# RWKV chain that keeps only the state's products: products with V and of the outputs moved into batches outside the chain

## The chip, the cores and the metric

One core of one Trainium2 chip runs the whole program, two chained transformer blocks. The metric is the time of one execution in microseconds (us) on the device; the median of several runs is taken. A core has a matrix engine (PE, TensorE), a vector engine (DVE), a scalar engine (ACT), a general engine (POOL) and a sequencer that starts most of the transfers (SP). Each runs its own list of instructions in order, and waits on semaphores where it needs another's result. A matmul writes into PSUM (8 banks of 128 partitions x 2 KB), from where DVE or ACT copy the result to SBUF.

## The reference, cut to what matters

Block 1 and the rest of block 2 are the same before and after. What the change touches is the RWKV-7 time mix of block 2: 8 heads of 64, two directions d, 512 tokens. Per head and direction a 64x64 state is carried over the tokens:

```
def step(state, inp):
    r_t, w_t, k_t, v_t, a_t, b_t = inp
    sa = jnp.einsum('dbhij,dbhj->dbhi', state, a_t)
    state = (state * w_t[..., None, :] + sa[..., :, None] * b_t[..., None, :]
             + v_t[..., :, None] * k_t[..., None, :])
    y = jnp.einsum('dbhij,dbhj->dbhi', state, r_t)
    return state, y
...
_, ys = lax.scan(step, s0, xs)
...
y = ys[0] + jnp.flip(ys[1], axis=1)
mu = jnp.mean(y, axis=-1, keepdims=True)
var = jnp.mean(jnp.square(y - mu), axis=-1, keepdims=True)
y = ((y - mu) * lax.rsqrt(var + GN_EPS)).reshape(bsz, t, c) * lnx_w + lnx_b
...
out = (y + bonus.reshape(bsz, t, c)) * g
```

## The kernel before, in words

`block2` does the scan in chunks of 64 tokens: 8 chunks, and 4 pairs of heads p = 0 to 3. The two heads of a pair, e = 0 and 1, lie on partitions 0 to 63 and 64 to 127. For each pair the program is written in four parts.

- `prep(p)` (from L1046) makes, from the projected r, k, v and gates, the chunk matrices: Z (128 columns a chunk: those of a and of r), BK (b and k), its transpose BKT, and the products pP = BK x Z (L1128, one matmul of 64 rows x 128 columns a chunk, head and direction), which DVE masks into M (L1130). So M holds what tokens of a chunk do to later ones of the same chunk. The strictly triangular blocks of M go out to memory (scL, L1135) and come back in another layout, as LF (L1150) and XH (L1152). There DVE inverts them: 30 rows, two instructions each (L1158 the products sx, L1160 their sum into XH). This is called the recursion below.
- fill: GEMM groups of later use (the gates of block 2, the next pair's projections, and for p = 3 the qkv projection, L1315), issued with low priority.
- `finish(p)` (from L1163) sends the inverses out (scX, L1169) and back into M (L1174), transposes (pax, L1182) and multiplies them together (pt1 L1189, pg2 L1194). LF's buffer holds its operand, so the LF of the next pair is loaded only when `finish(p)` is through.
- `chain(p)`: V is transposed (pvs, L1204) into VU, M x V of every chunk is made at once (pv, L1215), and 8 steps follow, one chunk a direction. A step is: pw = Z x state (L1229); DVE adds M x V (L1231, w); pu = M x w (L1234); ACT and DVE copy a head each into VU (L1000); then in px the old state times the identity (L1241) plus BKT x [V, U] (L1243); ACT scales one direction into the new state S (L1264), DVE the other (L1265). Each step also makes its output py from S and VU (L1250, L1252), copied by ACT (L1256) or added by DVE (L1258). Group norm, the gate and the store follow (to L1299).

A matmul of this f32 kind is one instruction in the program and two in the profile. The fills' and qkv's operands are float32r and are one in both.

What sets the order of the work: a list scheduler places all instructions of these parts, each engine's list apart, before the program runs, by priority, readiness by its own costs and free buffers. Fill has the lowest priority and goes where a chain's matmul is not ready. The order is fixed when the program is built. PSUM: pool `pg` (tag g, 2 banks) and `pa_` (tag a, 2), `ps_` (s, 2), `pc_` (y and c, one each). A qkv group needs both banks of g and both of a; `finish(p)` uses the banks of a (for p = 3 those of s).

Times below call f0, f1, f2, f3 the ends of the last pg2 matmul of each `finish` and "attention" the start of block 2's attention (paS, L1388).

Of the kernel before, what the change touches and what calls it, by code (L numbers as in the profile page):

```python
# [17 lines left out]
S = 512  # L18
# [138 lines left out]
class Ker:  # L157
# [806 lines left out]
    def block2(self, out):  # L964
# [79 lines left out]
        def prep(p):  # L1044
# [36 lines left out]
            for d in range(2):  # L1081
# [37 lines left out]
                for hf in ((0, 1), (1, 0))[d]:  # L1119
                    cs = slice(4 * hf, 4 * hf + 4)  # L1120
                    Z[hf] = rk.tile([128, 4, 128], F32, tag=f"Z{d}", name=f"Z{p}{d}{hf}", bufs=4)
                    nc.vector.tensor_tensor(Z[hf][:, :, 0:64], perm(kn, 64)[:, cs], perm(prv, 66)[:, cs], ALU.mult)
                    ve.tensor_tensor(Z[hf][:, :, 64:128], c8(r_)[:, cs], inc[:, cs], ALU.mult)  # L1123
                    for e in range(2):
                        rr = slice(64 * e, 64 * e + 64)
                        pp = ps_.tile([128, 4, 128], F32, tag="s", name=f"pP{p}{d}{hf}{e}")
                        for i in range(4):
                            nc.tensor.matmul(pp[:, i, :], BK[rr, 4 * hf + i, :], Z[hf][rr, i, :], start=True, stop=True)  # L1128
                        mk = rmask[d].rearrange("p (o t) -> p o t", o=2)[:, e:e + 1]
                        nc.vector.tensor_tensor(M[e][:, d, cs], pp, mk.to_broadcast([128, 4, 128]), ALU.mult)  # L1130
# [66 lines left out]
        def chain(p, st, u, PCs, XH, LF, M):  # L1197
            Y = rl.tile([128, 8, 64], F32, tag="Y", name=f"Y{p}")
            vt = V[p]
            VU = rl.tile([128, 8, 128], F32, tag="VU", name=f"VU{p}")  # L1200
            for h in range(2):
# [15 lines left out]
            Sn = None
            for s in range(8):
                cd = (s, 7 - s)
                zs = [st[d][0][cd[d] // 4][:, cd[d] % 4, :] for d in range(2)]  # L1220
                So = Sn
                pcb = pc_.tile([128, 512], F32, tag="c", name=f"pcb{p}{s}")
                pw, pu, px = [pcb[:, 128 * i:128 * i + 128].rearrange("p (d v) -> p d v", d=2) for i in range(3)]
                w = W0[:, 0, s, :]
                w = bass.AP(w.tensor, w.offset, [list(w.ap[0]), [512 + (7 - 2 * s) * 64, 2], [1, 64]])
                if s > 0:
                    for d in range(2):
                        for e in range(2):
                            nc.tensor.matmul(pw[O[e], d, :], zs[d][H[e], 0:64], So[H[e], d, :], start=True, stop=True)  # L1229
# [15 lines left out]
                def ymm():  # L1245
                    py = pc_.tile([128, 2, 64], F32, tag="y", name=f"py{p}{s}")
                    for d in range(2):
                        for e in range(2):
                            if s > 0:
                                nc.tensor.matmul(py[H[e], d, :], zs[d][H[e], 64:128], So[H[e], d, :], start=True, stop=False)  # L1250
                        for e in range(2):
                            nc.tensor.matmul(py[H[e], d, :], M[e][:, d, cd[d], 64:128], VU[:, cd[d], H[e]], start=s == 0, stop=True)  # L1252
                    b = Y[:, s, :]
                    yv = bass.AP(b.tensor, b.offset, [list(b.ap[0]), [(7 - 2 * s) * 64, 2], [1, 64]])
                    if s < 4:
                        nc.scalar.activation(yv, py, AF.Copy)  # L1256
                    else:
                        nc.vector.tensor_tensor(yv, py, yv, ALU.add)  # L1258
# [16 lines left out]
            yt = W0[:, 0].rearrange("p c v -> p (c v)")  # L1275
# [164 lines left out]
        st = prep(0)  # L1440
        fill(W[0], 5)
        finish(0, *st)
        chain(0, *st)
        st = prep(1)
        fill(W[1], 8)
        finish(1, *st)
# [185 lines left out]
```

## Time and profile before

| what | value |
|---|---|
| runs, median | 1834.92, 1851.11, 1856.5 us; 1851.11 us |
| profiled execution: time, span | 1853.1 us, 1851.3 us |
| PE busy, mean granted clock | 1763.1 us (95% of the span), 0.957 |
| DVE, ACT, POOL busy | 1108.2, 780.1, 207.6 us |
| f0, f1, f2, f3, attention | 945.2, 1016.8, 1122.7, 1210.7, 1276 us from the span's start |

In the rows, "busy" of an engine is the time that its instructions took, and x the number of instructions. PE overlaps its matmuls, so that a row's duration is longer than the distance to the next row's start: paces are read from start to start. PEclk is the granted clock as a share of 2.4 GHz: 1.00 is 2.4 GHz, 0.50 is 1.2 GHz, and values between are stretches with some of both. PEld are the weight loads beside the matmuls.

### The profile page before, as it was taken

Reading aid. Unit: us, or ns where it says so; the run is one execution under the profiler, and the core shown is the slowest. Engines: PE = TensorE matmul, PEld = TensorE weight load, DVE = VectorE, ACT = ScalarE, POOL = GpSimd, SP = SyncE. Lnnn points to the kernel's source line nnn. Section 1 sums busy time; section 2 is a strip of 40 time slices with the busy share of each in tenths; the row PEclk is TensorE's granted clock in tenths of the full one; section 3 lists DMA queues with packets and bytes.
Section 4 is the critical chain, followed back from the end, with each engine's and each line's share of the span. In section 5 each row is a group of like instructions: output and inputs, shape, how many; then the busy total and the mean of one; then the engine's idle time right before and its main releaser. Section 6 shows DMA issues by size and latency. Waiting matters only on the chain.

```text
span 1851.3 us, 30948 instructions
## 1 busy us (share of the span) xinstructions
PE 1763.1 (95%) x11888; PEld 1481.1 (80%) x11888; DVE 1108.2 (60%) x2311; ACT 780.1 (42%) x1559; POOL 207.6 (11%) x238
## 2 busy tenths in 40 slices
PE   8999989999999999897789998999999999999998
PEld 7787877889989999776667767876678888888887
DVE  5765786787734777855746682436556553355445
ACT  6552547654433446543233331235434442234333
POOL 1100130200000003442212121112000000000000
PEclk9999999999999999988689997689999999999999
DMA  5221324543333325622122122112055333333333
GB/s 170 59 52 47 83 54 154 160 126 92 92 97 92 92 86 164 179 68 58 46 66 58 44 63 71 39 33 92 18 185 157 103 93 96 97 91 97 96 92 131
DMA packets 130676, 170.83 MB, mean 92 GB/s; under 512 B 44456, under 2 KB 59056, under 8 KB 130529
## 3 DMA queue, kind: packets, MB, share of 16 engines
q1 hardware_dynamic: 130528, 168.87, 31.9%
q8 instruction: 93, 1.52, 0.3%
q14 instruction: 55, 0.44, 0.1%
HBM read 155.19 MB, written 13.63 MB: 91 GB/s over the span
## 4 chain that ended last, share of the span: by engine, by line
PE 83%; DVE 7%; DMA 4%; issue 3%; ACT 2%; POOL 1%; SPq 0%; DVEq 0%; POOLq 0%; ACTq 0%
PE ps_w_ff L251 19%; PE ps_w_ffn_in L251 13%; PE ps_w_in L284 6%; PE ps_w_in L251 6%; PE ps_w_ffn_out L251 6%; PE ps_qkv L1315 3%; PE ps_w_out L251 2%; PE pP L1128 2%; PE ps_w_ple_gate L251 2%; DMA XH<-scL 1%; PE ps_w_up_attn L251 1%; PE py L1252 1%; PE paS L1388 1%; PE ps_first L364 1%; PE ps_w_o L266 1%
## 5 line engine op out<-in xcount | busy, mean ns | idle before, releaser
L203 DVE TENSOR_TENSOR wl_w_ff<-raw_w_ff,wh_w_ff 128x512 fp32r<-128x512 f32 x128 | 88.2, 689 | 131.7 <-ACT wh_w_ff L202 131.6
L202 ACT ACTIVATE wh_w_ff<-raw_w_ff 128x512 fp32r<-128x512 f32 x128 | 80.9, 632 | 194.8 <-PE ps_w_ff L251 186.1
L203 POOL TENSOR_TENSOR wl_w_in<-raw_w_in,wh_w_in 128x512 fp32r<-128x512 f32 x60 | 81.9, 1370 | 260.0 <-ACT wh_w_in L202 191.8
L202 ACT ACTIVATE wh_w_in<-raw_w_in 128x512 fp32r<-128x512 f32 (+1 forms) x118 | 72.9, 622 | 89.9 <-PE ps_w_in L284 38.2
L202 ACT ACTIVATE wh_w_ffn_in<-raw_w_ffn_in 128x512 fp32r<-128x512 f32 x96 | 59.9, 630 | 101.5 <-PE ps_w_ffn_in L251 88.0
L251 PE MATMUL ps_w_ff<-Yl,wh_w_ff 128*128 128x512 f32 x256 | 101.0, 395 | 0.0
L251 PE MATMUL ps_w_ff<-Yh,wh_w_ff 128*128 128x512 f32 x256 | 101.0, 395 | 0.0
L251 PE MATMUL ps_w_ff<-Yh,wl_w_ff 128*128 128x512 f32 x256 | 101.0, 395 | 0.0
L251 PE MATMUL ps_w_ffn_out<-Y_hi,wl_w_ffn_out 128*128 128x256 f32 (+1 forms) x256 | 83.5, 326 | 2.2 <-DVE wl_w_ffn_out L203 2.1
L251 PE MATMUL ps_w_ffn_out<-Y_hi,wh_w_ffn_out 128*128 128x256 f32 (+1 forms) x256 | 83.7, 327 | 0.0
L251 PE MATMUL ps_w_ffn_out<-Y_lo,wh_w_ffn_out 128*128 128x256 f32 (+1 forms) x256 | 83.4, 326 | 0.0
L203 DVE TENSOR_TENSOR wl_w_ffn_in<-raw_w_ffn_in,wh_w_ffn_in 128x512 fp32r<-128x512 f32 x96 | 65.7, 689 | 20.4 <-ACT wh_w_ffn_in L202 19.4
L251 PE MATMUL ps_w_ffn_in<-fa_hi,wl_w_ffn_in 128*128 128x258 f32 x352 | 74.3, 285 | 2.0 <-DVE wl_w_ffn_in L203 2.0
L251 PE MATMUL ps_w_ffn_in<-fa_hi,wh_w_ffn_in 128*128 128x258 f32 x352 | 74.1, 285 | 1.9 <-ACT wh_w_ffn_in L202 1.9
L203 DVE TENSOR_TENSOR wl_w_ffn_out<-raw_w_ffn_out,wh_w_ffn_out 128x512 fp32r<-128x512 f32 (+1 forms) x72 | 47.4, 662 | 47.2 <-ACT wh_w_ffn_out L202 46.4
L251 PE MATMUL ps_w_ffn_in<-fb_hi,wl_w_ffn_in 128*128 128x258 f32 x352 | 74.3, 285 | 0.2 <-DVE wl_w_ffn_in L203 0.2
L251 PE MATMUL ps_w_ffn_in<-fb_lo,wh_w_ffn_in 128*128 128x258 f32 x352 | 74.4, 285 | 0.0
L251 PE MATMUL ps_w_ffn_in<-fb_hi,wh_w_ffn_in 128*128 128x258 f32 x352 | 74.4, 286 | 0.0
L251 PE MATMUL ps_w_ffn_in<-fa_lo,wh_w_ffn_in 128*128 128x258 f32 x352 | 74.2, 284 | 0.0
L202 ACT ACTIVATE wh_w_ffn_out<-raw_w_ffn_out 128x512 fp32r<-128x512 f32 (+1 forms) x72 | 41.5, 582 | 61.4 <-PE ps_w_ffn_out L251 45.6
L1128 PE MATMUL pP<-Z,BK 64*128 64x128 f32 x256 | 43.7, 354 | 16.7 <-DVE Z L1123 11.4
L251 PEld LDWEIGHTS ps_w_ffn_in<-fa_hi,wl_w_ffn_in 128*128 128x128 f32 x352 | 56.3, 191 | 2.4 <-DVE wl_w_ffn_in L203 2.4
(663 smaller groups left out, 5267.3 us busy)
## 6 DMA issues: line engine op xcount, KB each, us to landing
raw_w_ff<-in_w_ff SPq DMA_DIRECT2D x128, 256.0 KB
raw_w_in<-in_w_in SPq DMA_DIRECT2D x116, 256.0 KB
raw_w_ffn_in<-in_w_ffn_in SPq DMA_DIRECT2D x96, 256.0 KB
raw_w_ffn_out<-in_w_ffn_out SPq DMA_DIRECT2D x40, 256.0 KB
raw_w_o<-in_w_o SPq DMA_DIRECT2D x32, 256.0 KB
raw_w_ffn_out<-in_w_ffn_out SPq DMA_DIRECT2D x32, 192.0 KB
gtd<-gt SPq DMA_DIRECT2D x16, 256.0 KB
g<-gtd SPq DMA_DIRECT2D x16, 256.0 KB
```

The source lines that it names most:

```text
L202: a = nc.scalar.activation(hi, src, AF.Copy)
L203: v = (eng or nc.vector).tensor_tensor(lo, src, hi, ALU.subtract)
L251: mm = nc.tensor.matmul(ps[si][:ncol, :s1 - s0], a[:, k, :], bk[:, s0:s1], start=(ks == k0 and k == 0 and pi == 0), stop=(ks + k == kend - ...
L266: nc.tensor.matmul(ps[:ncol, :s1 - s0], a[:, k, :], b[kk // 4][:, kk % 4, s0:s1], start=first and k == 0 and n == 0, stop=not first and k ...
L284: nc.tensor.matmul(ps[:ncol, :s1 - s0], a[:, k, :], bk[:, s0:s1], start=(n == 0), stop=(n == 3 * kn - 1))
L364: nc.tensor.matmul(p[:ncol, :s1 - s0], a[:, k % 4, :], b[h][:, k % 4, s0:s1], start=(k == 0 and n == 0), stop=(k == 7 and n == 2))
L1128: nc.tensor.matmul(pp[:, i, :], BK[rr, 4 * hf + i, :], Z[hf][rr, i, :], start=True, stop=True)
L1252: nc.tensor.matmul(py[H[e], d, :], M[e][:, d, cd[d], 64:128], VU[:, cd[d], H[e]], start=s == 0, stop=True)
L1315: nc.tensor.matmul(pq[i][:, :256], l, r[:, k - ks, :], start=(k == 0 and n == 0), stop=(k == 7 and n == 2))
L1388: nc.tensor.matmul(pS[:, :128 * nk], qT[rr, j, 128 * n:128 * n + 128], kT[rr, 128 * b0:128 * b1], start=True, stop=True)
```

## The change

- In `prep`, the pP matmuls of the two heads alternate, into two PSUM tiles; before, four of one head came before four of the other. DVE masks both after.
- A new `pre`: V goes to its own tile VT; W0 = M x V (pv) is copied by ACT alone; a new batch pk = BKT x V of all chunks goes through two banks of tag a (s for p = 3), and DVE scales it by PC into PV.
- `chain` keeps pw, w, pu, the copy of U (one ACT instruction), and px, now BKT x U alone (4 matmuls). DVE makes the new state from px, in two instructions (one a direction), on top of t = PC x old state + PV, which are two more beside. No matmul with the identity, no copy of VU on DVE, no copy of S on ACT. The state of every step stays in PV's tile.
- All outputs come in one batch of 92 matmuls a pair into pya (tag y) and pyb (a bank of tag a, or s for p = 3); one ACT copy, one DVE addition into u's tile.
- `pair` calls the parts in the same order with the same fills.

```diff
                     ve.tensor_tensor(Z[hf][:, :, 64:128], c8(r_)[:, cs], inc[:, cs], ALU.mult)
+                    pps = [ps_.tile([128, 4, 128], F32, tag="s", name=f"pP{p}{d}{hf}{e}") for e in range(2)]
+                    for i in range(4):
+                        for e in range(2):
+                            nc.tensor.matmul(pps[e][:, i, :], BK[H[e], 4 * hf + i, :], Z[hf][H[e], i, :], start=True, stop=True)
                     for e in range(2):
-                        rr = slice(64 * e, 64 * e + 64)
-                        pp = ps_.tile([128, 4, 128], F32, tag="s", name=f"pP{p}{d}{hf}{e}")
-                        for i in range(4):
-                            nc.tensor.matmul(pp[:, i, :], BK[rr, 4 * hf + i, :], Z[hf][rr, i, :], start=True, stop=True)
...
+            PV = rl.tile([128, 2, 8, 64], F32, tag="PV", name=f"PV{p}")
             for d in range(2):
                 pv = pc_.tile([128, 8, 64], F32, tag="y", name=f"pv{p}{d}")
+                pk = pool.tile([128, 8, 64], F32, tag=tag, name=f"pk{p}{d}", bufs=2)
+                for c in range(8):
                     for e in range(2):
+                        nc.tensor.matmul(pv[O[e], c, :], M[e][H[e], d, c, 0:64], VT[H[e], c, :], start=True, stop=True)
+                    for e in range(2):
+                        nc.tensor.matmul(pk[H[e], c, :], bkt(d, c)[H[e], H[e]], VT[H[e], c, :], start=True, stop=True)
+                nc.scalar.activation(W0[:, d], pv, AF.Copy)
+                nc.vector.tensor_tensor(PV[:, d], pk, PCs[:, d, :].rearrange("p (c o) -> p c o", o=1).to_broadcast([128, 8, 64]), ALU.mult)
...
-                for e in range(2):
-                    b = VU[O[e], s, H[e]]
-                    ev(e, bass.AP(b.tensor, b.offset, [list(b.ap[0]), [(7 - 2 * s) * 128, 2], [1, 64]]), pu[O[e]])
-                if s < 7:
+                nc.scalar.activation(cross(U, s), pu, AF.Copy)
+                if s == 7:
+                    continue
+                base = [PV[:, d, cd[d], :] for d in range(2)]
+                if s > 0:
+                    t = rk.tile([128, 2, 64], F32, tag="S", name=f"S{p}{s}", bufs=2)
                     for d in range(2):
+                        nc.vector.scalar_tensor_tensor(t[:, d, :], prev(d, s), PCs[:, d, cd[d]:cd[d] + 1], base[d], ALU.mult, ALU.add)
+                    base = [t[:, d, :] for d in range(2)]
+                for d in range(2):
+                    for e in range(2):
+                        nc.tensor.matmul(px[H[e], d, :], bkt(d, cd[d])[O[e], H[e]], U[O[e], d, cd[d], :], start=True, stop=True)
+                for d in range(2):
+                    nc.vector.scalar_tensor_tensor(prev(d, s + 1), px[:, d, :], PCs[:, d, cd[d]:cd[d] + 1], base[d], ALU.mult, ALU.add)
+            pya = pc_.tile([128, 8, 64], F32, tag="y", name=f"pya{p}")
+            pyb = pool.tile([128, 8, 64], F32, tag=tag, name=f"pyb{p}", bufs=2)
...
+                for k in range(len(own[0])):
+                    for ps, ops in ((pya, own), (pyb, oth)):
                         for e in range(2):
-                            nc.tensor.matmul(px[H[e], d, :], st[d][1][cd[d] // 4][:, cd[d] % 4, H[e]], VU[:, cd[d], H[e]], start=s == 0, stop=True)
...
+                            if k < len(ops[e]):
+                                nc.tensor.matmul(ps[H[e], c, :], *ops[e][k], start=k == 0, stop=k == len(ops[e]) - 1)
+            nc.scalar.activation(Y, pya, AF.Copy)
+            nc.vector.tensor_tensor(Y, pyb, Y, ALU.add)
...
+        for p in range(3):
+            pair(p, lambda: fill(W[p], 5 + 3 * p))
+        pair(3, tail, ps_, "s")
```

How the change moves instructions, at three places. In these rows the first number is the place on the engine's list, then the line, the operation, what it writes and reads, and the shape; ps_w_in is fill.

PE, one step of pair 0's chain, before: pcb is pw, pu and px by line, py the outputs.

```order
5516 L1234 MATMUL pcb_10433<-w_10438,M_9716 64x64
...
5520 L251 MATMUL ps_w_in_17_11049<-hb_hi,wh_w_in_2293760_11070 128x512
5521 L251 MATMUL ps_w_in_17_11049<-hb_lo,wh_w_in_2293760_11070 128x512
5522 L1252 MATMUL py_10455<-VU_10326,M_9716 64x64
5523 L251 MATMUL ps_w_in_17_11049<-hb_hi,wl_w_in_2293760_11071 128x512
5524 L1241 MATMUL pcb_10433<-S_10420,cst 128x64
5525 L1243 MATMUL pcb_10433<-VU_10326,BKT_9777 64x64 x2
5526 L1241 MATMUL pcb_10433<-S_10420,cst 128x64
5527 L1243 MATMUL pcb_10433<-VU_10326,BKT_9849 64x64 x2
5528 L1252 MATMUL py_10455<-VU_10326,M_9717 64x64
5529 L1250 MATMUL py_10455<-S_10420,Z_9814 64x64 x2
```

And the same place of the change, where pcb is written by pw (L1241), pu (L1246) and px (L1258):

```order
5511 L1241 MATMUL pcb_10429<-PV_10344,Z_9741 64x64 x2
5512 L1241 MATMUL pcb_10429<-PV_10344,Z_9814 64x64 x2
5513 L251 MATMUL ps_w_in_10_11053<-hb_hi,wh_w_in_1376256_11074 128x512
5514 L251 MATMUL ps_w_in_10_11053<-hb_lo,wh_w_in_1376256_11074 128x512
5515 L251 MATMUL ps_w_in_10_11053<-hb_hi,wl_w_in_1376256_11075 128x512
5516 L1246 MATMUL pcb_10429<-w_10434,M_9716 64x64
...
5520 L251 MATMUL ps_w_in_10_11053<-hb_hi,wh_w_in_1376256_11074 128x512
5521 L251 MATMUL ps_w_in_10_11053<-hb_lo,wh_w_in_1376256_11074 128x512
5522 L1258 MATMUL pcb_10429<-W_10343,BKT_9777 64x64 x2
5523 L1258 MATMUL pcb_10429<-W_10343,BKT_9849 64x64 x2
```

A step has three short groups of four matmuls where it had four groups, one of them of 11, and the y matmuls are gone from it.

PE, pair 2's chain, in the change (ps_qkv is the fill there, W the tile that U is written into). Before, every step of this chain has ps_qkv between its groups, as the fill above.

```order
6246 L1327 MATMUL ps_qkv_12987<-wh_w_qkv_131072_13051,hb_hi 128x256
6247 L1327 MATMUL ps_qkv_12987<-wl_w_qkv_131072_13052,hb_hi 128x256
6248 L1327 MATMUL ps_qkv_12987<-wh_w_qkv_131072_13051,hb_lo 128x256
6249 L1241 MATMUL pcb_12468<-PV_12362,Z_11718 64x64 x2
6250 L1241 MATMUL pcb_12468<-PV_12362,Z_11791 64x64 x2
6251 L1246 MATMUL pcb_12468<-w_12473,M_11693 64x64
...
6254 L1246 MATMUL pcb_12468<-w_12473,M_11694 64x64
6255 L1258 MATMUL pcb_12468<-W_12361,BKT_11754 64x64 x2
6256 L1258 MATMUL pcb_12468<-W_12361,BKT_11826 64x64 x2
6257 L1241 MATMUL pcb_12489<-PV_12362,Z_11718 64x64 x2
```

From the third step to the end of this chain nothing stands between its groups but outputs of the batch near the end. The group of qkv needs a fourth PSUM bank, of tag a, and pyb holds it until its addition.

DVE, pair 0's chain, where the recursion of pair 1 (sx, XH) begins, before (w is a step's sum, VU the copy, S the state):

```order
1275 L1265 TENSOR_SCALAR S_10392<-pcb_10381,PC_9775 128x64
1276 L1014 TENSOR_TENSOR zt_9641<-ps_w_in_10_11006,rsh 128x512
1277 L1231 TENSOR_TENSOR w_10406<-pcb_10401,W_10344 128x128
1278 L1158 TENSOR_TENSOR sx_10830<-XH_10826,LF_10825 128x30
1279 L1026 TENSOR_TENSOR zs_11045<-zt_9641 128x512
1280 L1160 TENSOR_TENSOR XH_10826<-XH_10826,sx_10830 128x30
1281 L1000 COPY VU_10326<-pcb_10401 64x2x64
```

And in the change (with buffer names in full: S01 is t of pair 0, step 1):

```order
1274 L1260 SCALAR_TENSOR_TENSOR PV0_10344<-pcb00_10417,PC0_9775,PV0_10344 128x64 x2
1275 L1254 SCALAR_TENSOR_TENSOR S01_10441<-PV0_10344,PC0_9775 128x64 x2
1276 L1158 TENSOR_TENSOR sx11_10877<-XH1_10873,LF1_10872 128x30
1277 L1160 TENSOR_TENSOR XH1_10873<-XH1_10873,sx11_10877 128x30
1278 L1243 TENSOR_TENSOR w01_10434<-pcb01_10429,W00_10343 128x128
```

The first sx, which needs the transfer of LF, stands ahead of the w of step 1, where it stood between w and the copy of VU of that step.

## Rows read from the trace of the kernel before

**Rows 1.** The page: busy time of PE, and its granted clock in 40 slices.

```profile
PE 1763.1 (95%) x11888; PEld 1481.1 (80%) x11888; DVE 1108.2 (60%) x2311; ACT 780.1 (42%) x1559; POOL 207.6 (11%) x238
PEclk9999999999999999988689997689999999999999
```

**Rows 2.** Windows to f0, f1, f2, f3, attention: length, engines' busy, clock, DMA.

```profile
800.00:945.20 145.20, 121.43 (x721) 95.36 (x722) 87.73 (x165) 50.95 (x82) 37.87 (x32) 0.80 0.25 64
945.20:1016.80 71.60, 64.62 (x624) 44.30 (x624) 40.60 (x119) 21.09 (x45) 12.83 (x12) 0.93 0.21 56
1016.80:1122.70 105.90, 101.33 (x958) 75.96 (x957) 70.84 (x166) 38.69 (x72) 22.38 (x20) 0.98 0.22 56
1122.70:1210.70 88.00, 82.21 (x689) 66.81 (x687) 37.73 (x113) 19.80 (x46) 11.04 (x11) 0.65 0.20 51
1210.70:1276.00 65.30, 64.11 (x580) 49.85 (x580) 32.94 (x112) 25.66 (x60) 13.68 (x10) 0.95 0.18 56
```

**Rows 3.** Timeline, a step of pair 0's chain: start, duration, PE's line, tiles, shape.

```profile
987.97 0.27 PE L1229 MATMUL pcb<-S,Z 64*64 64x64 f32 x2
...
988.35 0.50 PE L251 MATMUL ps_w_in<-ha_hi,wl_w_in 128*128 128x512 f32 x1
...
988.69 0.40 PE L251 MATMUL ps_w_in<-hb_hi,wh_w_in 128*128 128x512 f32 x1
...
989.01 0.45 PE L1234 MATMUL pcb<-w,M 64*64 64x64 f32 x8
...
989.39 0.50 PE L251 MATMUL ps_w_in<-hb_lo,wh_w_in 128*128 128x512 f32 x1
...
989.73 0.40 PE L251 MATMUL ps_w_in<-hb_hi,wl_w_in 128*128 128x512 f32 x1
...
990.05 0.33 PE L1252 MATMUL py<-VU,M 128*64 128x64 f32 x2
...
990.31 0.50 PE L251 MATMUL ps_w_in<-hb_hi,wh_w_in 128*128 128x512 f32 x1
...
990.90 0.43 PE L1241 MATMUL pcb<-S,cst 128*128 128x64 f32 x2
...
992.81 0.50 PE L251 MATMUL ps_w_in<-hb_lo,wh_w_in 128*128 128x512 f32 x1
...
993.69 0.27 PE L1229 MATMUL pcb<-S,Z 64*64 64x64 f32 x2
```

**Rows 4.** Lines in 945 to 997: busy us, mean ns, idle before, releasers.

```profile
L1264 ACT ACTIVATE S<-pcb,PC 128x64 f32<-128x64 f32 x7 | 2.2, 314 | 21.4 <-PE pcb L1243 21.4
...
L1231 DVE TENSOR_TENSOR w<-pcb,W 128x128 f32<-128x128 f32 x7 | 2.0, 290 | 3.4 <-PE pcb L1229 3.4
```

**Rows 5.** Chain of waits, pieces: start, length, what (counts as in the profile).

```profile
1098.03 1.08 PE pP L1128 x8
1099.12 1.08 PE pv L1215 x32
...
1187.82 6.15 PE ps_qkv L1315 x32
...
1268.22 5.83 PE ps_w_in L251 x25
```

**Rows 6.** The same chain: the two transfers that it waits for.

```profile
946.34 13.10 DMA LF<-scL
...
1123.36 13.53 DMA XH<-scL
```

**Rows 7.** Windows, line L1158 (sx) alone: length, DVE busy, clock, DMA.

```profile
1048.00:1102.50 54.50, 12.20 (x30) 0.97 0.17 48
1136.00:1185.00 49.00, 8.94 (x30) 0.50 0.09 25
```

**Rows 8.** Windows in pair 2's chain, all engines, columns as in Rows 2.

```profile
1130.00:1140.00 10.00, 4.36 (x48) 3.44 (x47) 2.56 (x10) 1.85 (x4) 1.70 (x2) 0.73 0.38 103
...
1160.00:1170.00 10.00, 10.00 (x66) 8.04 (x67) 4.57 (x14) 3.00 (x7) 1.27 (x1) 0.50 0.01 2
```

More of the change, by code (lines that the diff above doesn't have):

```diff
@@ L1195, in finish, with pre @@
                 ev(e, M[e][R[e], :, :, 32:64], pg2_[R[e]])
-        def chain(p, st, u, PCs, XH, LF, M):
-            Y = rl.tile([128, 8, 64], F32, tag="Y", name=f"Y{p}")
+        def pre(p, st, u, PCs, M, pool=pa_, tag="a"):
             vt = V[p]
-            VU = rl.tile([128, 8, 128], F32, tag="VU", name=f"VU{p}")
+            VT = rl.tile([128, 8, 64], F32, tag="VT", name=f"VT{p}")
             for h in range(2):
@@ L1228, in chain @@
                         for e in range(2):
-                            nc.tensor.matmul(pw[O[e], d, :], zs[d][H[e], 0:64], So[H[e], d, :], start=True, stop=True)
+                            nc.tensor.matmul(pw[O[e], d, :], zc(d, cd[d])[H[e], 0:64], prev(d, s)[H[e]], start=True, stop=True)
                     w0, w = w, rk.tile([128, 2, 64], F32, tag="w", name=f"w{p}{s}", bufs=2)
@@ L1245, in ymm @@
[L1245 to L1258, printed above, removed]
@@ new lines, in chain @@
+                for d in range(2):
+                    nc.vector.scalar_tensor_tensor(prev(d, s + 1), px[:, d, :], PCs[:, d, cd[d]:cd[d] + 1], base[d], ALU.mult, ALU.add)
+            Y = u.rearrange("p (c v) -> p c v", c=8)
+            pya = pc_.tile([128, 8, 64], F32, tag="y", name=f"pya{p}")
+            pyb = pool.tile([128, 8, 64], F32, tag=tag, name=f"pyb{p}", bufs=2)
+            for c in range(8):
+                own, oth = [[], []], [[], []]
+                for d in range(2):
+                    s = (c, 7 - c)[d]
+                    for e in range(2):
+                        if s > 0:
+                            own[e].append((zc(d, c)[H[e], 64:128], prev(d, s)[H[e]]))
+                        own[e].append((M[e][H[e], d, c, 64:128], VT[H[e], c, :]))
+                        oth[e].append((M[e][O[e], d, c, 64:128], U[O[e], d, c, :]))
+                for k in range(len(own[0])):
+                    for ps, ops in ((pya, own), (pyb, oth)):
+                        for e in range(2):
+                            if k < len(ops[e]):
+                                nc.tensor.matmul(ps[H[e], c, :], *ops[e][k], start=k == 0, stop=k == len(ops[e]) - 1)
@@ L1274, in chain @@
             nc.vector.tensor_tensor(Y, Y, b8(m8), ALU.subtract)
-            yt = W0[:, 0].rearrange("p c v -> p (c v)")
+            yt = st[0][0][0].rearrange("p c t -> p (c t)")
             sq = yt.rearrange("p (c v) -> p c v", c=8)
@@ L1438, in fill, with pair, tail @@
                 low(gates, gq.pop(0))
[L1440 to L1446, printed above, removed]
-        chain(1, *st)
-        st = prep(2)
-        fill(W[2], 11)
-        finish(2, *st)
-        chain(2, *st)
-        st = prep(3)
-        low(qkv)
-        low(qknorm)
-        fill(W[3])
-        finish(3, *st, ps_, "s")
-        chain(3, *st)
+        def pair(p, mid, *where):
+            st, u, PCs, XH, LF, M = prep(p)
+            mid()
+            finish(p, st, u, PCs, XH, LF, M, *where)
+            x = pre(p, st, u, PCs, M, *where)
+            chain(p, st, u, PCs, M, *x, *where)
+        def tail():
+            low(qkv)
+            low(qknorm)
+            fill(W[3])
+        for p in range(3):
+            pair(p, lambda: fill(W[p], 5 + 3 * p))
+        pair(3, tail, ps_, "s")
         es1.close()
```

31 lines of the change are left out of this document (12 added, 19 removed).

## The prediction, made before the change had run

> **What bounds the kernel now.** I read the page first: PE is busy for 95% of the span [rows 1], so the program as a whole ends when PE has done its list. The row of granted clocks shows where it is not at full speed: slices 18 to 21 and 25 to 27 of 40, 46 us each, that is about 790 to 970 and 1110 to 1250 us. This is the RWKV part that the change edits. Windows over its stages [rows 2] separate two things. PE is without work for 7.0, 4.6, 5.8 and 1.2 us of the four stages from f0 to attention, 18.6 us of 330.8. And the stage f2 to f3 runs at a clock of 0.65; inside pair 2's chain ten microseconds are fully busy at 0.50, that is at 1.2 GHz [rows 8]. The chain of waits then names what holds PE where it does stand still: two transfers of the recursion's data, 13.1 and 13.5 us [rows 6].
>
> So two paths run beside each other. One is PE's list. The other is, for each pair, the transfer in, the recursion on DVE, the transfer out, `finish`, `chain`. DVE works 18 to 24 us on a recursion (the sx of pairs 2 and 3, half of it, take 12.20 and 8.94 us), yet the recursions last 54 and 49 us [rows 7], since its instructions stand on DVE's list between those of a chain, and wait with them.
>
> **What the change removes from PE, per pair.** A middle step of the chain, from start to start [rows 3]: pw with two outputs 0.38 us (987.97 to 988.35), pu 0.38 (989.01 to 989.39), an early output 0.26 (990.05 to 990.31), px with the identity and the outputs 1.91 (990.90 to 992.81): 2.93 us. The new step has three groups of four matmuls; each is taken as pu, 0.38, together 1.14. That is 1.79 us less in each of six middle steps; of the first and the last step, which lack a part, I take half, 0.9 each: 12.5 us. Going into and out of a group costs too. A fill matmul by itself takes 5.83/25 = 0.233 us [rows 5]; the one before a group lasts 0.32 (988.69 to 989.01), the first after one 0.34 (989.39 to 989.73), so 0.2 us a group. One group fewer in 8 steps: 1.6 us. Removed: 14.1 us.
>
> **What it adds.** The batch of outputs is 92 matmuls, 184 records. At the pace of pv, 32 in 1.08 us [rows 5], it takes 6.2 us. At half of that, if all four quarters of the array work beside each other, 3.1. The group of pw with outputs, 16 records in 0.38 us on four quarters, lies between: 0.024 us each, so 4.4. As the order puts pya and pyb beside each other only in places, I take 5. The batch pk is 64 records, 2.2 us at pv's pace, 1.1 at half; I take 2.2, as it stands in stretches of its own. Net per pair 14.1 - 7.2 = 6.9, between 5.7 and 9.9; four pairs 28 us, 23 to 40.
>
> **pP with alternating heads.** Eight records of 64x128 take 1.08 us, as much as 32 records of pv with 64 columns [rows 5]: double the columns, four times the time. pv's heads alternate and lie on different rows of the array, pP's do not. If alternation is what makes the difference, pP's 256 records go from 34.6 us (32 x 1.08) to half, 17.3 less. If it does nothing, zero. I take 13, since pv is the nearest row and some matmuls stand alone. The Trainium skill, TensorEngine Tiling (Array Packing), section Key Properties, states that different tiles can load and multiply in parallel; by it the sum would have the whole 17. No row of before shows two 64x128 tiles at once.
>
> So PE's list becomes some 41 us shorter at full clock, 23 to 57.
>
> **What of it lies on the path.** Stage by stage, by the orders shown:
> - To f0: nothing of the chain yet; a quarter of the pP gain: -3 us.
> - f0 to f1, 71.6 us. The transfer of LF, 13 us, remains, and the wait behind it grows: the first sx now stands ahead of w, so the chain stops one group earlier, for about 2 us more (the earlier hops of a step: pw to pu 1.04 us, pu to the next group 1.04 [rows 3]). After that a step takes 3 x 0.38 + 3 x 0.2 + 9 fills x 0.233 = 3.8 us against 5.72 (987.97 to 993.69). Its waits alone sum to about 3.4: two hops of 1.04, and px with two such DVE instructions and the way back, 1.3; so PE and waits are about even. Seven steps save 13 us, but the recursion among them still has to go through: 18 us of it, 10 of the chain's own DVE work at 1.3 a step (w 0.29 [rows 4] and four new instructions, which no row shows; the nearest is ACT's S of the same size, 0.31 [rows 4], and w, twice as wide, so 0.15 to 0.31 each, taken as 0.25), and about 4 of other work. It ends at 13 + 34 instead of 48, and transfers out and `finish` follow as before: -5 us.
> - f1 to f2, 105.9 us, of which DVE works 70.8 [rows 2]. The chain ends some 13 us sooner, but pair 2's pP moves into it, so LF comes later, and the recursion starts only behind the chain's last w: about f1 + 38, where it was f1 + 31 [rows 7]. From there DVE has 60 instructions of the recursion and some 40 others, about 41 us in place of 54, as no chain's steps stand among them and make it wait: -5 us.
> - f2 to f3, 88.0 us. 189 qkv matmuls filled it; now the fourth bank is held by pyb, 18 stand in the first two steps and 82 behind the outputs. Steps 2 to 7 run on waits alone, with sx between them on DVE: about 4.5 us each: the 3.4 of waits, more for small groups at half clock and for an sx that is under way. The recursion ends near f2 + 52 rather than + 62, and 26 us follow as before (1185 to 1210.7 [rows 7, 2]): -12 us.
> - f3 to attention, 65.3 us. Here PE is the bound (64.1 busy). It gets 10 more gate matmuls and 71 more of qkv, at 0.233 and 0.116 us 10.5 us in all, and loses 6.9: +4. Of this work 28 matmuls, 4.4 us, stood behind the start of attention before: in the sum -0.5.
>
> Together -26 us. On ACT and POOL nothing moves onto the path: ACT loses S and gains a wider copy of U. Against the profiled execution's own 1853.1 us (2 us above the median shown) this gives **1827 us**.
>
> **Rivals.**
> - *Path, not PE* (1838 to 1862, at 1848). The 41 us become idle time: PE waits for the same transfers and the same recursion. For it speak the 13 us transfers that nobody shortens, and DVE's load between f1 and f2. Against it, that PE was busy 92 to 98% of these stages, so work removed there does let later work in. Only f2 to f3 gives something, about 5 us: 1848.
> - *The whole gain* (1798 to 1815, at 1803). PE's 41 us arrive, and of the 31 us that f2 to f3 loses to the clock (88.0 x 0.35) some 9 come on top, the rest going into idle time there: 1853 - 41 - 9 = 1803. For it: the fills that cost double at half clock leave that stage.
> - *Slower: the clock falls and stays down.* Steps 2 to 7 of pair 2's chain leave PE mostly idle, and in these rows idle and low clock go together: 5.6 us idle in the window at 0.73, then 0.50 for fifty microseconds though busy throughout [rows 8]. The moved qkv work then comes in pair 3's chain, between the same short groups. If 32 us of its work run at 0.50, as pair 2's chain did, they cost 32 us more, and f2 to f3, with its small groups at half speed, loses its 12: 1827 + 44 = 1871. It decides if the clock is still 0.50 in the middle of pair 3's chain. Against it: 32 qkv matmuls in a row took 6.15 us before [rows 5], partly at the higher clock, so a run of them raises it, and 53 stand in a row behind the outputs. The Trainium skill, TensorE: Matmul & The Clock Gate, section "HAM oscillation — how this bites in real kernels", states that gaps in PE's work drop the clock to half and that what follows starts slow; the rows of before agree with it (0.73, then 0.50), and it speaks against this change.
> - *pP does not pair up.* Then f0 keeps its place and the other stages lose little, as they wait on DVE: 1831, inside the forecast.
>
> **Chances.** Forecast (1815 to 1838) 0.48, path 0.24, whole gain 0.15, slower (over 1862) 0.13. The range, 1802 to 1858, leaves out the ends of the two outer cases. A measurement of this kernel tells about 1% from no change, 18.5 us: faster means below 1832.6. That holds for the whole gain and for five sixths of the forecast: 0.55; over 1869.6 lies most of the slower case, 0.11; the rest is the same, 0.34.
>
> **What the profile after would show.** A middle step of pair 0's chain from pw to pw: 3.8 us; above 4.5 the waits rule it. Eight pP records in half of 1.08 us, or as before. The output batch of a pair in 3.1 to 6.2 us. f1, f2, f3 and attention at 66, 167, 243 and 312 us after f0 (before: 71.6, 177.5, 265.5, 330.8). PE idle near 12 us or more in pair 2's chain. The clock in pair 3's chain: near 1.00, or 0.50. The prediction is wrong if pair 2's recursion does not end earlier, since 12 of the 26 us hang on that, or if the clock stays down after it.

## The result, and the profile after

The changed kernel takes 1823.58 us (median of 16 runs, 1817.39 to 1833.56) against 1850.93 us before (16 runs). The ratio is 0.9854, 95% interval 0.9836 to 0.9873, so 27 us less. 1827 us was forecast, 1802 to 1858 as range. The profiled execution has a span of 1824.2 us against 1851.3.

The page's busy line and clock line of the changed kernel answer to [rows 1]:

```profile
PE 1705.5 (93%) x12304; PEld 1444.0 (79%) x12304; DVE 1117.0 (61%) x2347; ACT 767.3 (42%) x1521; POOL 206.7 (11%) x238
...
PEclk9999999999999999999789987899999999999999
```

PE's busy time fell by 57.6 us, more than twice what the program gained: PE now has more idle time. Windows over the same stages, to f0, f1, f2, f3 and attention (length, busy us of PE, PEld, DVE, ACT, POOL, clock, DMA), answer to [rows 2]; the last begins at the start of the last pg2 matmul, 0.2 us ahead of f3:

```profile
800.00:939.10 139.10, 111.97 (x738) 86.36 (x737) 89.06 (x166) 52.55 (x85) 38.74 (x33) 0.88 0.25 66
939.10:1003.70 64.60, 55.28 (x715) 39.41 (x713) 43.72 (x127) 15.21 (x30) 10.83 (x9) 0.93 0.23 63
1003.70:1122.70 119.00, 102.82 (x1101) 78.41 (x1101) 76.31 (x175) 37.45 (x67) 26.21 (x23) 0.89 0.22 57
1122.70:1183.90 61.20, 45.13 (x713) 38.80 (x713) 32.46 (x113) 12.72 (x27) 6.46 (x6) 0.77 0.19 48
1183.70:1254.80 71.10, 66.96 (x756) 54.84 (x753) 40.73 (x132) 28.50 (x63) 18.74 (x15) 0.98 0.23 69
```

f2 stands at 1122.7 us in both kernels. All that was won up to f1, 13 us, is lost again from f1 to f2 (119.0 where it was 105.9), and the gain of the whole is made between f2 and f3 (61.2 where it was 88.0).

A step of pair 0's chain after, PE's timeline, start and duration, answers to [rows 3]:

```profile
966.52 0.45 PE L1246 MATMUL pcb<-w,M 64*64 64x64 f32 x8
966.90 0.50 PE L251 MATMUL ps_w_in<-ha_hi,wl_w_in 128*128 128x512 f32 x1
...
967.56 0.45 PE L1258 MATMUL pcb<-W,BKT 64*64 64x64 f32 x8
...
969.07 0.45 PE L1241 MATMUL pcb<-PV,Z 64*64 64x64 f32 x8
...
970.34 0.45 PE L1246 MATMUL pcb<-w,M 64*64 64x64 f32 x8
```

From pu to pu 3.82 us, where 5.72 was read; a group takes 0.38 to the next fill. The chain of waits has a piece for pP, as [rows 5] had:

```profile
984.18 1.09 PE pP L1127 x16
```

Sixteen records take as long as eight did: the two heads do work beside each other.

Why f1 to f2 grew is seen on three engines. First SP's list, the transfers of pair 2's recursion:

```profile
1034.94 1.82 SPq L1135 DMA_DIRECT2D scL<-M  x4
1037.71 0.35 SPq L211 DMA_DIRECT2D raw_w_in<-in_w_in  x1
1038.23 0.56 SPq L1150 DMA_DIRECT2D LF<-scL  x1
1038.85 8.31 SPq L1152 DMA_DIRECT2D XH<-scL  x2
```

Then DVE's timeline, with the last mask of pair 2's M between two instructions of pair 1's chain, and the first sx of the recursion:

```profile
1033.85 0.47 DVE L1254 SCALAR_TENSOR_TENSOR S<-PV,PC 128x64 f32<-128x64 f32 x2
1034.23 0.68 DVE L1130 TENSOR_TENSOR M<-pP,cst 128x512 f32<-128x512 f32 x1
1035.05 0.29 DVE L1243 TENSOR_TENSOR w<-pcb,W 128x128 f32<-128x128 f32 x1
1035.26 0.68 DVE L1130 TENSOR_TENSOR M<-pP,cst 128x512 f32<-128x512 f32 x1
...
1053.14 0.19 DVE L1158 TENSOR_TENSOR sx<-XH,LF 128x30 f32<-128x30 f32 x1 [9.74 <-DMA XH<-scL]
```

The last M is ready at 1035.9 us, f1 + 32. Then come the transfers, out to memory (scL) and back (LF, XH), and the first sx waits for XH, the last of them. The recursion starts at f1 + 49; before, it started at f1 + 31 [rows 7]. In absolute time it starts 5 us later than before although f1 comes 13 us sooner.

Last, pair 2's chain without fill, a step on PE, DVE and ACT:

```profile
1143.02 0.70 PE L1241 MATMUL pcb<-PV,Z 64*64 64x64 f32 x8 [0.74 <-DVE PV L1260]
...
1143.75 0.29 DVE L1243 TENSOR_TENSOR w<-pcb,W 128x128 f32<-128x128 f32 x1 [0.32 <-PE pcb L1241]
...
1144.10 0.70 PE L1246 MATMUL pcb<-w,M 64*64 64x64 f32 x8 [0.38 <-DVE w L1243]
...
1144.84 0.28 ACT L1247 ACTIVATE W<-pcb 128x128 f32<-128x128 f32 x1 [3.30 <-PE pcb L1246]
...
1145.17 0.69 PE L1258 MATMUL pcb<-W,BKT 64*64 64x64 f32 x8 [0.38 <-ACT W L1247]
...
1145.98 0.48 DVE L1260 SCALAR_TENSOR_TENSOR PV<-pcb,PC,S 128x64 f32<-128x64 f32 x2 [0.56 <-PE pcb L1258]
...
1146.60 0.69 PE L1241 MATMUL pcb<-PV,Z 64*64 64x64 f32 x8 [0.74 <-DVE PV L1260]
```

and its clock in the chain, behind it in the batch of outputs, and in the qkv that follows (windows, columns as above):

```profile
1136.00:1156.00 20.00, 11.94 (x156) 9.33 (x158) 13.59 (x60) 1.66 (x6) 0.00 (x0) 0.50 0.00 1
1156.00:1163.00 7.00, 3.91 (x154) 3.77 (x150) 6.24 (x26) 0.60 (x1) 0.12 (x1) 0.85 0.02 5
1163.00:1183.90 20.90, 20.25 (x280) 17.80 (x281) 8.54 (x18) 9.90 (x18) 6.33 (x5) 1.00 0.43 105
```

The step takes 3.58 us at 1.2 GHz with PE waiting before every group: three hops of 1.07 to 1.43 us each, which are matmul, copy and the ways between.

### The profile page after: what moved, and what is told of

Read it like the earlier page. It is cut to its first block, busy times and chain, and to the rows that moved or that the text cites. A ratio compares the mean times of both kernels' runs of the same rounds, so it can differ in the third digit from the quotient of the medians.

```text
span 1824.2 us, 31816 instructions
## 1 busy us (share of the span) xinstructions
PE 1705.5 (93%) x12304; PEld 1444.0 (79%) x12304; DVE 1117.0 (61%) x2347; ACT 767.3 (42%) x1521; POOL 206.7 (11%) x238
## 4 chain that ended last, share of the span: by engine, by line
PE 44%; DVE 7%; DMA 3%; issue 3%; ACT 1%; POOL 0%; SPq 0%; DVEq 0%; ACTq 0%; POOLq 0%
PE ps_w_ff L251 20%; PE ps_w_in L251 5%; PE ps_w_out L251 2%; PE ps_w_ple_gate L251 2%; PE ps_qkv L1327 2%; DMA XH<-scL 2%; DMA LF<-scL 1%; PE pP L1127 1%; PE ps_w_up_rwkv L251 1%; PE ps_w_up_attn L251 1%; PE paS L1414 1%; PE paS L1400 1%; DVE XH L1160 1%; DVE sx L1158 1%; DVE BK L1117 1%
## 5 line engine op out<-in xcount | busy, mean ns | idle before, releaser
L251 PE MATMUL ps_w_ffn_in<-fa_hi,wl_w_ffn_in 128*128 128x258 f32 x352 | 74.3, 285 | 2.0 <-DVE wl_w_ffn_in L203 2.0
L251 PE MATMUL ps_w_ffn_in<-fb_hi,wl_w_ffn_in 128*128 128x258 f32 x352 | 74.3, 285 | 0.2 <-DVE wl_w_ffn_in L203 0.2
L251 PEld LDWEIGHTS ps_w_ffn_in<-fa_hi,wh_w_ffn_in 128*128 128x128 f32 x352 | 56.1, 190 | 2.2 <-ACT wh_w_ffn_in L202 1.9
```

The lines of the kernel that those rows point to most:

```text
L251: mm = nc.tensor.matmul(ps[si][:ncol, :s1 - s0], a[:, k, :], bk[:, s0:s1], start=(ks == k0 and k == 0 and pi == 0), stop=(ks + k == kend - ...
```

## The experiments

Stages of each profiled execution, us: f0, then the lengths to f1, f2, f3, attention, and from there to the end. Here f0 to f3 are read at the start of the last pg2 matmul, 0.2 us ahead of its end, so the stage to attention is 0.2 us longer than by the definition.

| kernel | f0 | to f1 | to f2 | to f3 | to attention | to the end |
|---|---|---|---|---|---|---|
| before | 945 | 71.6 | 105.9 | 88.0 | 66.4 | 574.4 |
| the change | 939 | 64.5 | 119.0 | 61.2 | 71.1 | 569.4 |
| e1 old chain, pP alternating | 937 | 75.1 | 105.6 | 86.5 | 66.3 | 573.3 |
| e2 new chain, pP apart | 942 | 67.1 | 131.2 | 60.7 | 74.3 | 571.8 |
| e3 change, bank free | 938 | 63.2 | 119.8 | 59.7 | 59.4 | 575.1 |
| e4 before, bank held | 949 | 75.5 | 109.7 | 72.8 | 81.1 | 569.7 |
| e5 change, prep lifted | 939 | 69.2 | 97.9 | 67.6 | 74.2 | 571.6 |
| e6 bank free, prep lifted | 937 | 68.9 | 97.8 | 66.6 | 61.7 | 569.9 |
| e7 bank free, smaller lift | 933 | 65.1 | 105.6 | 78.3 | 63.5 | 576.1 |
| e8 old chain, prep lifted | 938 | 90.7 | 81.5 | 126.9 | 76.4 | 568.8 |
| e9 as e6, pP apart | 951 | 68.6 | 103.3 | 65.0 | 59.2 | 571.0 |
| e10 as e6, recursion lifted | 933 | 64.7 | 91.8 | 92.2 | 57.8 | 571.0 |

Each row is one execution. How far it can be trusted shows where two programs are the same. Up to pair 0's first pP all twelve kernels have the same list on PE, and yet this pP starts between 815.5 us (e6) and 826.3 us (e4). e4's list on PE is that of the kernel before up to 1121 us there, just ahead of f2, and yet f0 comes 4.3 us later, and the stages to f1 and f2 are each some 4 us longer. So a difference of 4 us in one stage, or of some 10 us in where a stage ends, shows nothing by itself.

Each "Ratio" below is the run's time to that of the kernel before, measured beside it, over several executions; the bracket is the 95% interval.

Two theories after the result. "Withheld fill": f2 to f3 became short because qkv stayed out of pair 2's chain. "Shorter steps": it became short because the chain has less in it, and what was withheld only left PE idle. And for f1 to f2: "prep inside the chain" against "DVE's work".

**e1, the pairing of pP alone.** In the kernel before:

```diff
+                    for i in range(4):
+                        for e in range(2):
+                            nc.tensor.matmul(pps[e][:, i, :], BK[H[e], 4 * hf + i, :], Z[hf][H[e], i, :], start=True, stop=True)
```

> The kernel before with one part of the change alone: the pP matmuls of the two heads alternate, into two PSUM tiles. Theory 'PE's list': eight pP records take half of 1.08 us, some 15 us of PE work go, and as PE is busy 92 to 98% of these stages the time falls by 8 to 13 us (ratio to before 0.993 to 0.996). Theory 'path': the pairing works, but only the stretch up to f0 gets shorter (the change ends f0 6.1 us sooner); f0 to attention keeps its 331 us, and the time falls by 4 to 6 us (ratio 0.997). If two tiles do not work beside each other: no change in f0, ratio 1.000.

Ratio 0.9926 (0.9902 to 0.9949): 14 us, so half of the change's gain comes with these lines alone. The size is that of "PE's list", and the interval excludes the 0.997 of "path". Where it comes is less sure. In the profile f0 comes 8.3 us sooner, f1, f2 and attention 5 to 7, the end 7.7, which looks like "path"; but half of all pP records, 128 of 256, stand ahead of f0 (pairs 0 and 1), so that "PE's list" has 8.7 us there as well, and what the other half gives in the stages behind can't be told from the 4 us by which equal stages differ.

**e2, the change without that pairing.**

```diff
-                    for i in range(4):
-                        for e in range(2):
...
+                    for e in range(2):
...
+                        for i in range(4):
+                            nc.tensor.matmul(pp[:, i, :], BK[rr, 4 * hf + i, :], Z[hf][rr, i, :], start=True, stop=True)
```

> The change with its pP matmuls as before (four of one head, then four of the other), all else kept. Theory 'path': f0 comes 5 to 6 us later than in the change, and the rest keeps its length: ratio to before 0.988 to 0.989 where the change has 0.985. Theory 'PE's list': 15 us of PE work come back, ratio 0.991 to 0.993.

Ratio 0.9975 (0.9951 to 1.0). Both theories missed: the new chain alone gives about 5 us, at most 9 (by the medians, 1845.34 against 1853.2, 8), and the pairing is worth some 22 us on top of it (14 to 30 by the two intervals, not measured side by side), where PE can save 17. The table shows where: f1 to f2 takes 131.2 us, 12 more than with the pairing, as pair 2's recursion starts at f1 + 55 in place of f1 + 49 and lasts 55 us in place of 47.

**e3, pair 2's outputs through one bank of their own.** The bank of tag a stays free for qkv:

```diff
+            if p == 2:
+                batch((pya, own))
+                nc.scalar.activation(Y, pya, AF.Copy)
+                pyb = pc_.tile([128, 8, 64], F32, tag="y", name=f"pyb{p}")
+                batch((pyb, oth))
```

> The change, but pair 2's outputs go through the bank of tag y alone, one half after the other, so that no bank of tag a is held in its chain; by the order qkv then fills every step of that chain, 183 matmuls from f2 to f3 where the change has 100. Theory 'withheld fill': what made f2 to f3 27 us shorter is that the chain ran without qkv at 1.2 GHz; with it steps take 5.5 to 6.5 us instead of 3.6, f3 comes 10 to 20 us later, attention some 5 to 10 us later: ratio to before 0.988 to 0.991. Theory 'shorter steps': the withheld fill only left PE idle (16 of 61 us from f2 to f3); with it back, work moves forward and the time falls by 5 to 9 us: ratio 0.980 to 0.983.

Ratio 0.9794 (0.9767 to 0.9822), below the change's interval. "Withheld fill" falls: with 183 qkv matmuls in it f2 to f3 takes 59.7 us, no more than the change's 61.2 with 100. Windows of this kernel from f2 on, columns as above:

```profile
1121.30:1126.00 4.70, 4.70 (x73) 4.52 (x72) 2.06 (x3) 0.28 (x1) 0.00 (x0) 0.50 0.26 58
1126.00:1131.00 5.00, 5.00 (x55) 4.05 (x53) 1.78 (x9) 0.85 (x2) 1.27 (x1) 0.95 0.13 52
1131.00:1136.00 5.00, 1.60 (x23) 1.20 (x21) 1.03 (x7) 0.63 (x1) 1.26 (x1) 1.00 0.47 133
1136.00:1141.00 5.00, 5.00 (x42) 4.21 (x41) 3.19 (x14) 0.91 (x2) 1.27 (x1) 0.66 0.02 3
1141.00:1146.00 5.00, 5.00 (x55) 4.20 (x56) 3.72 (x17) 2.86 (x7) 0.01 (x1) 1.00 0.18 52
```

PE idles 3.4 us behind the transfer of LF, goes on at 0.66, and is at 2.4 GHz five microseconds later, in the middle of the chain. Its steps there, PE's timeline:

```profile
1143.07 0.45 PE L1241 MATMUL pcb<-PV,Z 64*64 64x64 f32 x8
...
1144.12 0.45 PE L1246 MATMUL pcb<-w,M 64*64 64x64 f32 x8
...
1145.16 0.45 PE L1258 MATMUL pcb<-W,BKT 64*64 64x64 f32 x8
...
1146.57 0.45 PE L1241 MATMUL pcb<-PV,Z 64*64 64x64 f32 x8
```

A step takes 3.50 us with 15 qkv matmuls in it, at 2.4 GHz, and 3.58 without any in the change, at 1.2 GHz. So the chain is no slower with the fill than it was without, and fill held back is paid for later: attention starts at 1240.4 us, in the change at 1254.8.

**e4, the kernel before with the bank held.**

```diff
+                if p == 2 and s == 0:
+                    hold = pa_.tile([128, 8, 64], F32, tag="a", name="hold", bufs=2)
+                    nc.tensor.matmul(hold[H[0], 0, :], st[0][1][0][:, 0, H[0]], VU[:, 0, H[0]], start=True, stop=True)
...
+                for s in (0, 7):
+                    nc.vector.scalar_tensor_tensor(Y[H[0], s, :], hold[H[0], 0, :], 0.0, Y[H[0], s, :], ALU.mult, ALU.add)
```

> The kernel before, with one bank of tag a held through pair 2's chain by a small matmul whose result is read, times zero, at the end of that chain. By the order 112 qkv matmuls instead of 189 stand between f2 and f3, and steps 3 to 7 have no fill. Theory 'withheld fill': this alone gives a good part of the change's gain from f2 to f3: that stage falls from 88 to 68 to 75 us, and the time by 8 to 15 us (ratio to before 0.992 to 0.996). Theory 'shorter steps': the steps without fill are little shorter, PE idles, the qkv work comes later: ratio 1.000 to 1.004.

Ratio 0.9984 (0.9956 to 1.0012), nearest to "shorter steps". The stage does fall to 72.8 us, but the next takes 81.1 in place of 66.4: withheld fill is a loan.

**e5, the change with prep lifted ahead of the chain before it.**

```diff
         def prep(p):
+            tc.cur_priority -= 2000
             st = {}
...
+            tc.cur_priority += 2000
             for t in range(1, 31):
```

> The change, with the priority of every prep (not of its recursion) lifted ahead of the chain of the pair before. By the order all products M of pair 2 then stand ahead of pair 1's chain on DVE, where in the change half of them stand between its steps. Theory 'prep inside the chain': f1 to f2 grew from 106 to 119 us because pair 2's last M came 32 us after f1, so LF landed at f1 + 49; now it lands by f1 + 30, f1 to f2 takes 98 to 108 us, and the time falls 8 to 13 us below the change's: ratio to before 0.978 to 0.981. Theory 'DVE's work': DVE has the same work ahead of f2 in any order, so f2 stays at 1119 to 1124 us and the ratio at 0.983 to 0.987. f0 and f1 may come a little later, as fill moves up.

Ratio 0.982 (0.9782 to 0.9859). Its stage windows from f1 on:

```profile
1008.60:1106.60 98.00, 92.67 (x983) 69.08 (x979) 73.43 (x169) 33.08 (x58) 19.62 (x18) 0.90 0.23 59
1106.60:1174.20 67.60, 48.50 (x766) 40.27 (x762) 33.55 (x115) 14.88 (x31) 6.56 (x7) 0.77 0.19 46
1174.20:1248.40 74.20, 67.42 (x775) 56.18 (x773) 44.18 (x131) 28.14 (x62) 18.19 (x14) 0.96 0.24 74
```

For f1 to f2 "prep inside the chain" is shown: 98 us, within its 98 to 108, pair 2's recursion starts 28 us after f1, and f2 comes at 1106.6, where "DVE's work" had 1119 to 1124. The time follows only in part. Of the 21 us won in this stage the others give most back: f0 to f1 is 4.7 us longer, f2 to f3 6.4, the last two 3.1 and 2.2. Behind f2, pair 3's last M now come right ahead of `finish(2)`, its recursion starts 18 us after f2 in place of 14, and the withheld qkv work waits behind it as before. The ratio's interval overlaps that of the change, so it is not settled that the lift alone gains anything over it.

**e6, both.** The lift of e5 in the kernel of e3:

```diff
+            tc.cur_priority -= 2000
...
+                pyb = pc_.tile([128, 8, 64], F32, tag="y", name=f"pyb{p}")
```

> The same lift of prep in the version that leaves pair 2's bank of tag a free. Theory 'prep inside the chain': the two gains add, 6 us of the free bank and 8 to 13 of the lift: ratio to before 0.972 to 0.975. Theory 'DVE's work': as the free bank alone, 0.978 to 0.981.

Ratio 0.9755 (0.9716 to 0.9794), median 1805.1 us: faster than both kernels, at the edge of what "prep inside the chain" said. The profiled span, 1802.2 us, is 22 below the change's; e3 had 9 of it, e5 4. That does not show that the lift is worth more where the bank is free: e6's execution was 8.7 us ahead of e3's at the first pP already, where both are still the same program, and by the ratios the lift is worth some 6 us alone and 7 with the bank free. Its interval overlaps that of e3, so that it beats the change is measured, that it beats e3 is not settled by these runs.

**e7, a smaller lift**, against e6:

```diff
-            tc.cur_priority -= 2000
+            tc.cur_priority -= 400
```

> As the last, with a smaller lift: half of pair 2's M stand ahead of pair 1's chain, the rest between its first steps, and recursions begin inside the chains. Theory 'prep inside the chain': LF of pair 2 lands between f1 + 30 and f1 + 40, so the ratio lies between the free bank alone and the full lift: 0.974 to 0.978. Theory 'DVE's work': 0.978 to 0.981.

Ratio 0.9835 (0.9803 to 0.9867): by its value worse than the free bank alone, though the intervals overlap, and neither theory's. f1 to f2 is shorter, 105.6 us, as expected, but the order puts part of pair 3's prep behind f2 (11 of its 32 pP matmuls), and f2 to f3 takes 78.3.

**e8, the old chain with alternating pP and the lift.** Against e1:

```diff
         def prep(p):
+            tc.cur_priority -= 2000
             st = {}
```

> The old chain (identity, outputs in every step) with alternating pP and the same lift of prep as in the first of these runs. It tells what the new chain itself is worth once prep no longer stands between its steps. Theory 'prep inside the chain': the old chain loses nothing to prep, so the lift gives it at most 3 us: ratio 0.990 to 0.994, 10 us or more above the new chain with the lift. Theory 'the order was what counted': the lift gives the old chain as much as the new one, 8 us or more: ratio 0.984 to 0.989.

Ratio 1.0211 (1.017 to 1.0252). Both missed. The lift left half of pair 3's pP behind f2 there, and the clock of that stage stayed low, with PE busy throughout from 1160 us on; a stretch of it:

```profile
1170.00:1200.00 30.00, 30.00 (x203) 24.35 (x203) 12.28 (x49) 5.63 (x15) 2.67 (x3) 0.50 0.06 19
```

Since another order of prep came with it, it doesn't tell what the new chain is worth by itself.

**e9, the best version with pP apart.** The edit of e2 in e6:

```diff
-                    for i in range(4):
-                        for e in range(2):
...
+                    for e in range(2):
...
+                        for i in range(4):
```

> The best version so far (bank free, prep lifted), with pP's matmuls as before the change: four of one head, then four of the other. Alternation was worth 22 us in the change and 14 alone; PE saves at most 17 us by it at full clock. Theory 'it also shortens the path': in the change pP stood inside pair 1's chain and ahead of LF, so each us of it counted twice; with prep ahead of the chain that is gone, and pP is worth 9 to 14 us: ratio to before 0.980 to 0.983. Theory 'PE's list': all 17 us or more, as PE's idle time is small here: ratio 0.985 to 0.988.

Ratio 0.9848 (0.9788 to 0.9908), median 1819.68 against 1805.1 of e6, not measured side by side: 14 to 17 us. The value is that of "PE's list". In the profile f0 comes 14 us later (951 for 937), but 5.5 of these lie ahead of the first pP, where nothing differs; the 8 that are left fit the half of the pP records that stands there. The intervals touch, so the size is open: by their ends it is anything from nothing to 35 us.

**e10, the recursion lifted too.** In `pair`, in place of the lift inside `prep`:

```diff
+            tc.cur_priority -= 2000
             st, u, PCs, XH, LF, M = prep(p)
+            tc.cur_priority += 2000
```

> As the best version, but the recursion is lifted with prep, ahead of the chain's steps on DVE. By the order the recursions end inside the chains, with four to six of its instructions between two instructions of the chain, where three or four stood. Theory 'the recursion sets f': f2 and f3 come 3 to 8 us earlier, ratio to before 0.971 to 0.975. Theory 'the chain's steps pay': steps get 0.6 to 1.2 us longer and the chains end later, ratio 0.977 to 0.981.

Ratio 0.9842 (0.9759 to 0.9924), not told apart from e6 or from the change. The recursion does set f2 (f1 to f2 91.8 us, f2 at 1089.7); but 24 of pair 3's 32 pP matmuls come behind f2, and f2 to f3 takes 92.2.

## Why the prediction was right, and where it was not

1827 us was forecast and 1823.58 came out. That the two lie so near is in good part luck: f1 to f2 was forecast 18 us too short and f2 to f3 15 us too long, and these two misses cancel. The other steps held in their direction and nearly in their size.

- **PE's list.** 41 us less at full clock, 23 to 57, were worked out; PE's busy time fell by 57.6, which counts the higher clock too. The terms that can be read: the step 3.82 us for 3.8; pP 16 records in 1.09 us for half of 1.08 each eight; pair 1's batch of outputs some 4.8 us (1042.6 to 1047.4) for 5. The statement of the Trainium skill, TensorEngine Tiling (Array Packing), section Key Properties, that different tiles multiply in parallel was weighed against a trace that did not show it, and 13 of its 17 us were taken; the trace after agrees with it in full, 1.09 us for 16.
- **To f0, f0 to f1.** -3 forecast, -6.1 measured; -5 forecast, -7.0 measured. The first term was read wrongly: not a quarter but half of the pP records stand ahead of f0, in the kernel before as well, which would have made it -6.5. Pair 1's recursion ended at f0 + 44, where 47 was taken.
- **f1 to f2, the step that failed.** "The recursion starts only behind the chain's last w: about f1 + 38", and -5 us was the result. The last w did come at f1 + 39, but the recursion's data were not there: it started at f1 + 49, behind the transfer of XH, and the stage grew by 13. The order was read rightly, half of pair 2's M inside pair 1's chain; what was not worked out is the time of that last M, f1 + 32, as steps with two or three wide prep instructions in them took longer than those of pair 0 (4.8 us against 4.1 on average), and the 17 us of transfers from it to the first sx. These 11 us are the larger part of the 18 that the term is off. e5 shows this cause: with prep ahead of the chain the recursion starts at f1 + 28 and the stage takes 98 us. Another 6 us are the recursion itself, which took 47 us from there where 41 was taken; why is not shown, though in e5 it took 38.
- **f2 to f3, mis-sized.** -12 us forecast, -26.8 measured. The steps took 3.58 us where 4.5 was taken, half clock and sx together costing 0.2 over the waits of 3.4; the recursion ended at f2 + 41 for + 52, and the way from there to f3 took 20 us for 26.
- **f3 to attention and on.** +4 and -4.4 forecast; +4.7 (70.9 against 66.2, as paS starts at 1276.9 us in the kernel before and not at the 1276 of its table) and -5.0 measured. The second agreement is weak: of the 28 matmuls that were to move ahead of attention the trace shows only the ten of fill, 2.3 us. All of qkv stands ahead of it in both kernels.

Of the rivals, "path, not PE" held up to f2 and nowhere after. "Slower: the clock falls and stays down" had its first half: the clock was 0.50 in pair 2's chain. It did not decide, since pair 3's stage ran at 0.98. The prediction's reason, that the run of qkv behind the outputs raises the clock, is not what happened: the clock was back at 1158.1 us, while PE worked through the batch of outputs, and that qkv began at 1163.0. The statement of the Trainium skill, TensorE: Matmul & The Clock Gate, section "HAM oscillation — how this bites in real kernels", that gaps in PE's work drop the clock, spoke against the change; the first half of this trace agrees with it (PE idle for 8 of 20 us in pair 2's chain, at 0.50). The stage's cost was PE idle for 16 us of 61, and in e3 it is 4.5 of 59.7. "The whole gain" was right that f2 to f3 gives the most; its 1803 us came only with the further edits of e6.

What the 27 us are made of is shown in part. 14 us come with pP alone (e1, 9 to 18 by its interval) and 5 with the new chain alone (e2, 0 to 9). By the middle values 9 us come only with both together; at the far ends of the two intervals nothing is left over, so that they give more than their sum is likely and not settled. That pP stood inside pair 1's chain, so that unpaired it also delays the recursion, fits e2's f1 to f2 of 131.2 us; e9 does not settle it, since pP was worth about as much there, 14 to 17 us, as alone.

## What to carry to other kernels

Work taken out of a chain lets everything behind it move up, also what the next chain is waiting for: look whether the next input's preparation now stands between the chain's steps, and try it ahead of them. Time that as well: it shortened the stage here by 21 us and the whole by far less (e5), and with the old chain the same lift cost 3% (e8 against e1). A bank that is held through a chain is a cost to the fill, not to the chain; give a batch a bank that the fill doesn't use. And a small edit beside the large one (here the order of 32 matmuls a pair) can be half of the gain: time it alone.

## What the runs showed of the hardware

The old chain with qkv between its steps stayed at 1.2 GHz for fifty microseconds although PE was busy all that time by the profile. [Rows 8] show a part of it before, and e1's windows again:

```profile
1140.00:1150.00 10.00, 10.00 (x73) 7.95 (x72) 3.83 (x16) 1.80 (x5) 1.27 (x1) 0.50 0.01 2
1150.00:1160.00 10.00, 10.00 (x63) 7.90 (x62) 3.24 (x13) 1.34 (x4) 0.00 (x0) 0.50 0.09 26
1160.00:1170.00 10.00, 10.00 (x75) 7.93 (x74) 3.52 (x14) 2.53 (x6) 1.33 (x1) 0.50 0.09 28
```

The new chain with the same fill was back at 2.4 GHz within five microseconds (e3). So a PE that is busy all the time by the profile can stay at the low clock. Why the new chain came back is not shown: the identity matmuls and the outputs of the old groups were not tried apart, and PE had also been idle for less ahead of it, 3.4 us in e3 against 6.4 in e1 (to 1133.8).

On DVE an sx, 0.26 us in the median, took 1.30 while POOL split a weight tile (the change, from 1055.93):

```profile
1055.93 1.26 POOL L203 TENSOR_TENSOR wl_w_in<-raw_w_in,wh_w_in 128x512 fp32r<-128x512 f32 x1 [3.15 <-issue]
1055.99 1.30 DVE L1158 TENSOR_TENSOR sx<-XH,LF 128x78 f32<-128x78 f32 x1
```

It ends 0.1 us behind POOL's instruction. Of the recursion's instructions of pair 2 before, eight took longer than 0.5 us, 8.5 us together, and each of the eight overlaps an instruction of POOL and ends 0.05 to 0.13 us behind it. Six of them are sx, 6.4 us of the 12.20 in [rows 7]; of pair 3's 30, 8.94 us in all, only two are as long. No run took POOL's work away.
